# Retention of four heads among the other heads' query and gate products, in a one-core diffusion block

## The chip, the cores and the metric

The kernel runs on one NeuronCore of a Trainium2 chip. The metric is the device time of one execution in microseconds (us). The kernel before took 1373.80, 1377.99 and 1381.97 us in three runs, a median of 1377.99. In what follows PE is TensorE, DVE is VectorE, ACT is ScalarE, POOL is GpSimd, and SP is the engine that issues most DMAs.

## What is computed

One layer of a hybrid backbone over 1024 tokens of width 1024, with 256 context tokens, in float32:

```python
hx = modulate(rmsnorm(x, norm1_g), mx[0], mx[1])       # mx: six vectors of silu(c) @ w_ada
ux = hx @ w_in                                         # 3 x 512 Hyena + 4 x 512 retention columns
x0, x1, v = split(short_conv(ux[:, :1536]))            # 3 taps
y_hy = bidir_long_conv(v * x1, h, bias) * x0           # by FFT, filter h from a small MLP
q, k, vr, g = split(ux[:, 1536:], 4)                   # 8 heads x 64
q, k = rope(q), rope(k / 8)                            # pairs of neighbouring columns rotated
o = retention(q, k, vr, forward) + retention(..., backward)   # chunks of 128 tokens
y_ret = groupnorm(o) * silu(g)
x = x + mx[2] * (concat(y_hy, y_ret) @ w_out)
x = x + mx[5] * (relu(modulate(rmsnorm(x)) @ w1) ** 2 @ w2)   # the MLP, and a final rmsnorm
```

## The kernel before

Every large float32 product is done in three passes, `mm3`: each operand is split into a rounded part and a rest (`hxh`, `hxl` for the normalised input, `wh`, `wl` for weights), and high times high, high times rest and rest times high are summed in PSUM. `slab` loads a slab of 256 columns of `w_in` in two DMAs, rounds it on ACT (`A.copy`) and makes the rest on DVE; there are two buffers for `wh` and two for `wl`, so a slab's cast waits for the products of the slab before the last. `prefetch` calls it for the next slab of a list (`cols`).

A slab's product is either token-major (`token_major`: 8 token blocks x 8 x 3 = 192 matmuls of 256 columns, the weights moving) or feature-major (`feature_major`: 96 matmuls of 512 columns, the tokens moving). K, V, q and g are token-major here, the convolution inputs x1, vh and x0 are feature-major.

The code is a sequence of stages, and a scheduler lays each engine's instructions into one fixed queue: by place in the code as buffers and data allow, while what stands in `urgent()` counts as 6000 places earlier. On the chip each engine runs its own queue strictly in order, and SP issues its DMAs in order, each waiting for what its row names.

The stages, by time in the profile: 97 to 249 us K, V, filter and context; 249 to 331 the inputs of convolution half hv0; 331 to 429 the transform of hv0 with the inputs of hv1 beside it; 429 to 509 the transform of hv1 with the gate products (`pgt`) beside it; 509 to 557 the query products (`pq`); 557 to 573 a change of buffers, in which the pool of `hxh` and `hxl` is freed and one called `big` opened; 573 to 655 retention; then the second half of the output projection, and the MLP.

A transform runs through 8 residues: forward products `pXv`, a multiplication by the filter on DVE, inverse products `pGv`, copied into `Gs` by ACT. Behind the last, DVE does the inverse butterflies into `yy`. Then, for each of two blocks and two halves, `vxl` and `x0l` are loaded from memory, ACT scales `vxl`, DVE adds `yy` and multiplies by `x0l`, and SP stores the result to `mix_d`. `modulation` computes an eighth of the modulation vectors: 8 loads `adaw`, 8 DVE operations into `adac`, 4 small products `pada`.

In the retention stage `retention(hh, n, ...)` does chunk n of heads 4 hh to 4 hh + 3. It loads q rotated by `rope` (`q2l`), keys, values and states; four PE transposes (`pqd`) turn q; DVE multiplies it by decay weights (`qw`) and ACT copies it into zero-padded tiles (`sgqz`); two products give the scores (`psc`); DVE masks them (`sT`, with the masks in `tabq`); 16 narrow products (`po`) sum `vtl` with `sT` and states `stl` with `qw`. After each second chunk `out_conv` adds the convolution's share of a 128-row block of the output projection (`poh`, 24 matmuls); it reads `mx`, which `split_mix` makes from `mix_d` through `mraw`. `group_norm` follows each four chunks.

## Time and profile before

| | |
|---|---|
| median of three runs | 1377.99 us |
| the profiled execution, its own time | 1370.97 us |
| its span | 1369.2 us |
| mean granted PE clock, of full speed | 0.98 |
| busy: PE, DVE, ACT, POOL | 95%, 71%, 39%, 1% |
| chain that ended last: PE, DVE, DMA, ACT | 77%, 8%, 7%, 4% |

PE is the engine that is nearly always busy, so the span is its work and its gaps. Weight loads (PEld) overlap the matmuls. The idle time of another engine costs nothing as long as PE has a matmul that can run.

### The profile page before, as it was taken

Reading aid. Unit: us, or ns where it says so; the run is one execution under the profiler, and the core shown is the slowest. Engines: PE = TensorE matmul, PEld = TensorE weight load, DVE = VectorE, ACT = ScalarE, POOL = GpSimd, SP = SyncE. Lnnn points to the kernel's source line nnn. Section 1 sums busy time; section 2 is a strip of 40 time slices with the busy share of each in tenths; the row PEclk is TensorE's granted clock in tenths of the full one; section 3 lists DMA queues with packets and bytes.
Section 4 is the critical chain, followed back from the end, with each engine's and each line's share of the span. In section 5 each row is a group of like instructions: output and inputs, shape, how many; then the busy total and the mean of one; then the engine's idle time right before and its main releaser. Section 6 shows DMA issues by size and latency. Waiting matters only on the chain.

```text
span 1369.2 us, 20105 instructions
## 1 busy us (share of the span) xinstructions
PE 1294.8 (95%) x7386; PEld 1083.1 (79%) x7386; DVE 973.3 (71%) x1721; ACT 533.6 (39%) x912; POOL 19.4 (1%) x24
## 2 busy tenths in 40 slices
...
GB/s 374 175 151 160 233 206 212 79 228 129 169 120 215 206 162 155 270 243 182 104 96 64 251 306 326 348 302 300 238 123 232 338 321 190 193 201 185 199 79 62
DMA packets 139570, 278.19 MB, mean 203 GB/s; under 512 B 14672, under 2 KB 47056, under 8 KB 137040
## 3 DMA queue, kind: packets, MB, share of 16 engines
...
q14 instruction: 40, 0.33, 0.1%
HBM read 193.75 MB, written 83.10 MB: 202 GB/s over the span
## 4 chain that ended last, share of the span: by engine, by line
PE 77%; DVE 8%; DMA 7%; ACT 4%; issue 2%; SPq 1%; POOL 0%; DVEq 0%; ACTq 0%; POOLq 0%
PE px L184 6%; PE px L185 6%; PE px L183 6%; PE pw L183 5%; PE py L183 5%; PE py L185 5%; PE py L184 5%; PE pw L185 5%; PE pw L184 5%; DMA dft_f_k<-in_dft_f 2%; PE pga L397 1%; PE pq L185 1%; PE pq L184 1%; PE pq L183 1%; PE pGv L901 1%
## 5 line engine op out<-in xcount | busy, mean ns | idle before, releaser
L1191 DVE TENSOR_TENSOR mt<-tr,mt 128x512 fp32r<-128x512 f32 x112 | 76.6, 688 | 99.6 <-ACT mt L1190 99.4
L1190 ACT CAST mt<-tr 128x512 fp32r<-128x512 f32 x112 | 69.6, 621 | 123.5 <-PE py L185 67.1
L183 PE MATMUL px<-mt,mw 128*128 128x512 f32 (+1 forms) x320 | 112.5, 352 | 3.0 <-ACT mw L1190 2.4
L184 PE MATMUL px<-mt,mw 128*128 128x512 f32 (+1 forms) x320 | 112.5, 352 | 0.7 <-DVE mt L1191 0.7
L185 PE MATMUL px<-mt,mw 128*128 128x512 f32 (+1 forms) x320 | 111.6, 350 | 0.0
L1191 DVE TENSOR_TENSOR mw<-wr,mw 128x512 fp32r<-128x512 f32 x112 | 76.6, 686 | 4.8 <-ACT mw L1190 4.4
L183 PE MATMUL py<-mt,mw 128*128 128x512 f32 x192 | 74.7, 389 | 0.0
L184 PE MATMUL py<-mt,mw 128*128 128x512 f32 x192 | 74.7, 389 | 0.0
L185 PE MATMUL py<-mt,mw 128*128 128x512 f32 x192 | 74.7, 389 | 0.0
L1190 ACT CAST mw<-wr 128x512 fp32r<-128x512 f32 x112 | 69.0, 617 | 9.8 <-DMA wr<-in_w_mlp 5.5
L183 PEld LDWEIGHTS px<-mt,mw 128*128 128x128 f32 x320 | 61.1, 191 | 11.4 <-ACT mw L1190 2.8
L184 PEld LDWEIGHTS px<-mt,mw 128*128 128x128 f32 x320 | 61.1, 191 | 9.2 <-DVE mt L1191 1.2
L185 PEld LDWEIGHTS px<-mt,mw 128*128 128x128 f32 x320 | 60.9, 191 | 8.2 <-DVE mw L1191 0.3
L183 PE MATMUL px<-hxh,wh_x 128*128 128x512 f32 x128 | 50.7, 396 | 0.0
L184 PE MATMUL px<-hxl,wh_x 128*128 128x512 f32 x128 | 50.6, 395 | 0.0
L185 PE MATMUL px<-hxh,wl_x 128*128 128x512 f32 x128 | 50.6, 395 | 0.0
L712 DVE SCALAR_TENSOR_TENSOR adac<-adaw,cs,adac 128x512 f32<-128x512 f32 x56 | 42.9, 766 | 9.8 <-DMA adaw<-in_w_ada 9.2
L185 PE MATMUL pk<-wh_k,hxl 128*128 128x256 f32 x128 | 39.2, 307 | 3.3 <-DVE hxl L438 3.3
L184 PEld LDWEIGHTS py<-mt,mw 128*128 128x128 f32 x192 | 36.0, 188 | 7.5
L183 PEld LDWEIGHTS py<-mt,mw 128*128 128x128 f32 x192 | 36.0, 188 | 7.5
L185 PEld LDWEIGHTS py<-mt,mw 128*128 128x128 f32 x192 | 36.0, 188 | 7.4
L183 PE MATMUL pk<-wh_k,hxh 128*128 128x256 f32 x128 | 39.6, 310 | 0.4 <-ACT hxh L434 0.4
...
## 6 DMA issues: line engine op xcount, KB each, us to landing
tr<-t_d SPq DMA_DIRECT2D x112, 256.0 KB, 4.0
adaw<-in_w_ada SPq DMA_DIRECT2D x64, 256.0 KB, 4.0
WH<-in_w_mlp SPq DMA_DIRECT2D x16, 1024.0 KB, 7.4
s_d<-WH SPq DMA_DIRECT2D x16, 1024.0 KB, 5.0
wr<-s_d SPq DMA_DIRECT2D x64, 256.0 KB, 4.0
wr<-in_w_mlp SPq DMA_DIRECT2D x48, 256.0 KB, 4.2
t_d<-c SPq DMA_DIRECT2D x40, 256.0 KB, 4.1
t_d<-CH SPq DMA_DIRECT2D x40, 256.0 KB, 5.4
```

The lines of the kernel that those rows point to most:

```text
L183: PE.matmul(o, lhsT=lh, rhs=rh, start=first, stop=False, **kw)
L184: PE.matmul(o, lhsT=lh, rhs=rl, start=False, stop=False, **kw)
L185: PE.matmul(o, lhsT=ll, rhs=rh, start=False, stop=last, **kw)
L397: PE.matmul(pga[h][0:4, n, :], lhsT=cv[:, k, :], rhs=w_[:, n * 512:(n + 1) * 512], start=(k == 0), stop=(k == KC - 1 and i == 1))
L712: V.scalar_tensor_tensor(ac, wa, cs[:, k, 0:1], ac, op0=ALU.mult, op1=ALU.add)
L901: PE.matmul(o, lhsT=y[:, 0, cb], rhs=iv[:, sl[0]], start=True, stop=False)
L1190: A.copy(hi, src)
L1191: V.tensor_tensor(lo, src, hi.bitcast(F32), op=ALU.subtract)
```

## The change

**Layout.** The host permutes the columns of q and k in a head, so that rotation pairs are 32 columns apart and not neighbours. q and g become feature-major. q is then rotated by `rotate`: four DMAs of 32 x 1024 swap the halves, three DVE operations of 128 x 1024 follow, and the result goes to `q_d`. Retention loads q feature-major, twice, into rows 0 to 63 and rows 64 to 127, so the transposes and the zero-padded copies go. The scores are four products over 64 rows, in two PSUM banks.

**Order.** The convolution is cut into `conv_in` (x1, vh), `conv_gate` (x0), `conv_dft` (transforms and inverse butterflies) and `conv_out` (the loads, DVE steps and stores behind them). All five modulation pieces that stood in this region, three of them beside the gate products, stand in the convolution; `vxl` takes the buffers of another tag (`bfy`). Slabs from the seventh on are loaded from GpSimd's queue instead of SP's. After the convolution come the products of q0 and g0, then heads 0 to 3 (`heads(0, ...)`), with q1 and g1 in eight pieces of 24 matmuls, one behind each chunk. Then the pools change, and heads 4 to 7 (`heads(1, ...)`) run with one `out_conv` of 24 matmuls behind each chunk. The normed result of heads 0 to 3 goes through memory (`y_d`).

```diff
+    rc = np.concatenate([cs, cs], axis=1)
+    rs = np.concatenate([-sn, sn], axis=1)
+    c["ropeT"] = np.ascontiguousarray(np.stack([np.tile(rc.T, (2, 1)), np.tile(rs.T, (2, 1))], 1))
...
+    w = v["w_in"][0].copy()
+    for c0 in (QC, KCOL):
+        w[:, c0:c0 + 512] = w[:, c0:c0 + 512].reshape(D, NH, 32, 2).transpose(0, 1, 3, 2).reshape(D, 512)
+    a["w_in"] = w.reshape(KC, P, -1, 256).transpose(2, 1, 0, 3)
...
-            SP.dma_start(raw, src[:, ks])
+            (SP if nxt[0] < 6 else G).dma_start(raw, src[:, ks])
...
-        cols += [("x1", hv, X1C + 256 * hv), ("vh", hv, VHC + 256 * hv), ("x0", hv, X0C + 256 * hv)]
-    cols += [("g", 0, GC), ("g", 1, GC + 256), ("q", 0, QC), ("q", 1, QC + 256)]
+        cols += [("x1", hv, X1C + 256 * hv), ("vh", hv, VHC + 256 * hv)]
+    cols += [("x0", hv, X0C + 256 * hv) for hv in range(2)]
+    for hh in range(2):
+        cols += [("q", hh, QC + 256 * hh), ("g", hh, GC + 256 * hh)]
...
+    def conv_out(hv, yy):
         for b in range(2):
             blk = 2 * hv + b
             yv = yy[:, b].rearrange("p c n -> p (c n)")
             for q in range(2):
                 cc = slice(q * 512, q * 512 + 512)
-                vx = cvp.tile([P, 512], F32, tag="fx", bufs=2, name=f"vxl{blk}{q}")
+                vx = cvp.tile([P, 512], F32, tag="bfy", bufs=2, name=f"vxl{blk}{q}")
...
+    yy0 = conv_dft(0, conv_in(0))
+    for _ in range(2):
+        modulation()
+    vT1 = conv_in(1)
+    for _ in range(2):
+        modulation()
+    conv_gate(0)
+    modulation()
+    with urgent():
+        conv_out(0, yy0)
+    conv_gate(1)
+    yy1 = conv_dft(1, vT1)
+    with urgent():
+        conv_out(1, yy1)
...
-    for hh in range(2):
-        for g, ps in token_major(("g", hh), f"pgt{hh}"):
-            sg = scp.tile([P, 4, 256], F32, tag="sc", bufs=3, name=f"sg{hh}{g}")
-            with urgent():
-                A.activation(sg, ps, AF.Silu)
-                SP.dma_start(sg_d[hh][g], sg.rearrange("p n d -> p (n d)"))
-            if hh + g < 2:
-                modulation()
-        prefetch()
...
-    for hh in range(2):
-        for g, ps in token_major(("q", hh), f"pq{hh}"):
...
+    def rotate(hh, b, qf):
+
+        qs = scp.tile([P, T], F32, tag="sc", bufs=3, name=f"qs{hh}{b}")
+        for i in range(4):
+            SP.dma_start(qs[32 * i:32 * i + 32], qf[32 * (i ^ 1):32 * (i ^ 1) + 32])
+        V.tensor_tensor(qs, qs, rot[:, 1], op=ALU.mult)
+        V.tensor_tensor(qf, qf, rot[:, 0], op=ALU.mult)
+        V.tensor_tensor(qf, qf, qs, op=ALU.add)
+        SP.dma_start(q_d[hh][b * P:(b + 1) * P], qf)
+
+    def last_products():
+
+        for kind in "qg":
+            wh, wl = slabs.pop((kind, 1))
+            for b in range(2):
+                o = scp.tile([P, T], F32, tag="sc", bufs=3, name=f"{kind}f1{b}")
+                for h in range(2):
+                    ps = ps_cv(f"p{kind}1{b}{h}")
+                    cc = slice(512 * h, 512 * h + 512)
+                    for k in range(KC):
+                        mm3(ps, wh[:, k, b * P:(b + 1) * P], wl[:, k, b * P:(b + 1) * P], hxh[k][:, cc], hxl[k][:, cc],
+                            k == 0, k == KC - 1)
+                    with urgent():
+                        if kind == "q":
+                            A.copy(o[:, cc], ps)
+                            if h:
+                                rotate(1, b, o)
+                        else:
+                            A.activation(o[:, cc], ps, AF.Silu)
+                            SP.dma_start(sg_d[2 + b][:, cc], o[:, cc])
+                    yield
...
+    for b, ps in feature_major(("q", 0), "pq0"):
         with urgent():
+            qf = scp.tile([P, T], F32, tag="sc", bufs=3, name=f"qf0{b}")
+            A.copy(qf, ps)
+            rotate(0, b, qf)
+    prefetch()
+    for b, ps in feature_major(("g", 0), "pgt0"):
+        with urgent():
+            sg = scp.tile([P, T], F32, tag="sc", bufs=3, name=f"sg0{b}")
+            A.activation(sg, ps, AF.Silu)
+            SP.dma_start(sg_d[b], sg)
...
+    def retention_tables(new):
+        ctrs, sgs, tabq = [new(nm) for nm in ("ctrs", "sgs", "tabq")]
+        SP.dma_start(tabq.rearrange("p a n -> p (a n)"), tab_d.rearrange("p a h n -> p (a h n)"))
...
-        q2 = rtl.tile([P, 4, 2 * HD], F32, tag="q2", bufs=2, name=f"q2l{nm}")
-        SP.dma_start(q2.rearrange("p h d -> p (h d)"), q2_d[hh][n])
+        rtl, rtp, wqT, msk = [rt[i] for i in ("l", "p", "wqT", "msk")]
+
+        q2 = rtl.tile([P, 4, P], F32, tag="q2", bufs=2, name=f"q2l{nm}")
+        for r in range(2):
+            SP.dma_start(q2[64 * r:64 * r + 64], q_d[hh].rearrange("(h d) t -> d h t", h=4)[:, :, n * P:(n + 1) * P])
...
-        pq = ps_aux(f"pqd{nm}")
-        for h in range(4):
-            PE.transpose(pq[:, h * P:(h + 1) * P], q2[:, h], ident)
-        pqv = pq.rearrange("p (h c) -> p h c", h=4)
         qw = rtp.tile([P, 4, P], F32, tag="qw", bufs=2, name=f"qw{nm}")
-        V.tensor_tensor(qw, pqv, wqT[:, hs], op=ALU.mult)
-        qT = qz[n % 2]
-        A.copy(qT[0:64, 0:4:2], pqv[0:64, 0:4:2])
-        A.copy(qT[64:128, 1:4:2], pqv[64:128, 1:4:2])
-        pc = ps_aux(f"psc{nm}")
+        V.tensor_tensor(qw, q2, wqT[:, hs], op=ALU.mult)
+
+        pc = ps_cv(f"psc{nm}0"), ps_aux(f"psc{nm}1")
         for pr in range(2):
-            PE.matmul(pc[:, pr * 256:(pr + 1) * 256], lhsT=kt[:, pr],
-                      rhs=qT[:, 2 * pr:2 * pr + 2].rearrange("p h c -> p (h c)"), start=True, stop=True)
+            for s in range(2):
+                rows = slice(64 * s, 64 * s + 64)
+                PE.matmul(pc[s][:, pr * P:(pr + 1) * P], lhsT=kt[rows, pr], rhs=q2[rows, 2 * pr + s],
+                          start=True, stop=True)
         sT = rtp.tile([P, 4, P], F32, tag="sT", bufs=2, name=f"sT{nm}")
-        V.tensor_tensor(sT, pc.rearrange("p (h c) -> p h c", h=4), msk[:, hs], op=ALU.mult)
+        for s in range(2):
+            V.tensor_tensor(sT[:, s:4:2], pc[s][:, 0:256].rearrange("p (h c) -> p h c", h=2),
+                            msk[:, 4 * hh + s:4 * hh + 4:2], op=ALU.mult)
...
+            V.scalar_tensor_tensor(sg[:, pr], pt, gn, sg[:, pr], op0=ALU.mult, op1=ALU.mult)
+            if hh == 0:
+                SP.dma_start(y_d[pr][g], sg[:, pr])
+            else:
+                split_ret(g, blk, sg[:, pr])
...
+    def heads(hh, more):
+
+        pending = None
         for g in range(2):
-            ctr = ctrs[:, g]
-            gss = rtp.tile([P, 4, 4], F32, tag="gss", bufs=2, name=f"gss{hh}{g}")
+            ctr = rt["ctr"][:, g]
+            gss = rt["p"].tile([P, 4, 4], F32, tag="gss", bufs=2, name=f"gss{hh}{g}")
             for j in range(4):
                 retention(hh, 4 * g + j, ctr, gss)
...
                 if j == 1 and pending:
                     group_norm(*pending)
                 if j == 1:
...
+                    sg = rt["sg"][:, 2 * g:2 * g + 2]
+                    for pr in range(2):
+                        SP.dma_start(sg[:, pr], sg_d[2 * hh + pr][:, 512 * g:512 * g + 512])
+                more(g, j)
             pending = hh, g, sg, ctr, gss
-    group_norm(*pending)
+        group_norm(*pending)
...
+    open_retention()
+    retention_tables(lambda nm: rt["l" if nm == "tabq" else "p"].tile([P, 4, 512], F32, name=f"{nm}0"))
+    products = last_products()
+
+    def last_heads(g, j):
+        next(products)
+        if (g, j) == (1, 3):
+            next(products, None)
+
+    heads(0, last_heads)
+    cpool("rtp")
...
+    for k in range(4):
+        split_mix(k)
+    for d in range(KC):
+        SP.dma_start(xn[d], I["xT"][d * P:(d + 1) * P])
+
+    def projection(g, j):
+        out_conv(4 * g + j)
+        if (g, j) == (0, 1):
+            wo.append(o2)
+            for a in range(2):
+                hi, lo, raw = [t[:, 2 * a:2 * a + 2] for t in (*o2, mraw)]
+                SP.dma_start(raw, I["w_out"][2][:, 2 * a:2 * a + 2])
+                A.copy(hi, raw)
+                V.tensor_tensor(lo, raw, hi.bitcast(F32), op=ALU.subtract)
+        if (g, j) == (0, 3):
+
+            wo.append(wpool.tile([P, 4, 512], F32, tag="wh", bufs=2, name="o3r"))
+            SP.dma_start(wo[1], I["w_out"][3])
+        if (g, j) in ((0, 2), (1, 0)):
+            for i in range(2):
+                raw = mraw[:, 2 * (j // 2) + i]
+                SP.dma_start(raw, y_d[i][g])
+                split_ret(g, i, raw)
...
+    wo = []
+    heads(1, projection)
```

How this moves instructions, at three places. A row is one instruction in its engine's queue, with output and inputs; behind `waits` are the semaphores of the queues and engines it waits for.

PE, from the last gate product of its stage on. Before, the gates' last group (`pgt11`) is followed by four groups of q products (`pq00` to `pq11`) and the projection (`poh0`):

```order
L184 MATMUL pgt11_4865<-wl_g1_4117,hxh7_398 128x256
L185 MATMUL pgt11_4865<-wh_g1_4116,hxl7_406 128x256
L183 MATMUL pq00_4975<-wh_q0_4724,hxh0_391 128x256
L184 MATMUL pq00_4975<-wl_q0_4725,hxh0_391 128x256
...
L185 MATMUL pq00_4975<-wh_q0_4724,hxl7_406 128x256
L183 MATMUL pq01_5088<-wh_q0_4724,hxh0_391 128x256
...
L185 MATMUL pq11_5324<-wh_q1_4965,hxl7_406 128x256
L183 MATMUL poh0_5600<-mx00_5465,wh_o0_5201 128x512
```

Now the last product of g0 (`pgt01`) is followed by the scores and the output of chunk 0 of heads 0 to 3, and the first piece of q1 (`pq100`) stands behind these:

```order
L189 MATMUL pgt01_4746<-hxl7_406,wh_g0_4209 128x512
L190 MATMUL pgt01_4746<-hxh7_398,wl_g0_4210 128x512
L1105 MATMUL psc0_00_4835<-q2l0_0_4823,ktl0_0_4826 128x128
L1105 MATMUL psc0_01_4836<-q2l0_0_4823,ktl0_0_4826 128x128
...
L1117 MATMUL po0_0_4844<-vtl0_0_4828,sT0_0_4841 64x64 x2
L1117 MATMUL po0_0_4844<-stl0_0_4830,qw0_0_4833 64x64 x2
...
L188 MATMUL pq100_4868<-hxh0_391,wh_q1_4684 128x512
L189 MATMUL pq100_4868<-hxl0_399,wh_q1_4684 128x512
```

So the cover of four groups of products between gate and retention has moved behind the first chunk.

SP, around the last stores of the mixed channels (`mix_d`). Before, the stores of q follow, and the masks (`tabq`) and retention's first loads (`q2l0_0`) come many issues later:

```order
L982 DMA mix_d3_2963<-vxl30_4441 128x512 [waits DMAHW5_49,DVE_49]
L976 DMA vxl31_4449<-vx_d3_2959 128x512 [waits DMAHW6_49,DMAHW2_49]
L982 DMA mix_d3_2963<-vxl31_4449 128x512 [waits DMAHW1_49,DVE_49]
L1009 DMA q2_d0_4459<-q200_5072 128x2x512 [waits DVE_49]
L1009 DMA q2_d0_4459<-q202_5080 128x2x512 [waits DMAHW3_49,DVE_49]
...
L1036 DMA tabq_5463<-tab_d_1411 128x2048 [waits DMAHW2_49]
L1055 DMA mraw_5471<-mix_d0_2960 128x512 [waits DMAHW3_49]
L1055 DMA mraw_5471<-mix_d0_2960 128x512 [waits DMAHW5_49]
...
L1079 DMA q2l0_0_5499<-q2_d0_4459 128x512 [waits DMAHW0_49]
L1055 DMA mraw_5471<-mix_d3_2963 128x512 [waits DMAHW1_49,DVE_49]
```

Now masks and loads stand right behind the last two stores, which wait for DVE:

```order
L1030 DMA q_d0_4556<-qf01_4673 128x1024 [waits DMAHW7_49,DVE_49]
L992 DMA mix_d2_2962<-vxl20_4519 128x512 [waits DMAHW1_49,DVE_49]
L992 DMA mix_d2_2962<-vxl21_4527 128x512 [waits DMAHW2_49,DVE_49]
L986 DMA vxl30_4535<-vx_d3_2959 128x512 [waits DMAHW5_49,DMAHW1_49]
L986 DMA vxl31_4543<-vx_d3_2959 128x512 [waits DMAHW6_49,DMAHW2_49]
L1065 DMA sg_d1_4553<-sg01_4795 128x1024 [waits DMAHW7_49,Activation_49]
L992 DMA mix_d3_2963<-vxl30_4535 128x512 [waits DMAHW0_49,DVE_49]
L992 DMA mix_d3_2963<-vxl31_4543 128x512 [waits DVE_49]
L1077 DMA tabq0_4820<-tab_d_1411 128x2048 [waits PE_49]
L1090 DMA q2l0_0_4823<-q_d0_4556 64x4x128 [waits DMAHW3_49]
L1092 DMA ktl0_0_4826<-kT_d0_1413 128x256 [waits DMAHW5_49]
```

What moved: the masks' load has now nothing between it and the end of the convolution's output.

ACT, around the scaling of `vxl`. Before, at the end of the gate products, the first half of slab q1 is cast between a silu and the scaling for block 3:

```order
L994 ACTIVATE sg10_4831<-pgt10_4734 128x1024 [waits DMAHW2_49,PE_49,Activation_49]
L979 ACTIVATE vxl21_4433<-vxl21_4433,cols_89 128x512 [waits DMAHW3_49,DMAHW5_49,DMAHW1_49,DVE_49]
L994 ACTIVATE sg11_4962<-pgt11_4865 128x1024 [waits PE_49,Activation_49]
L206 CAST wh_q1_4965<-wr_q10_4967 128x1024 [waits DMAHW7_49]
L979 ACTIVATE vxl30_4441<-vxl30_4441,cols_89 128x512 [waits DMAHW4_49,DMAHW7_49,DMAHW1_49,DVE_49]
L206 CAST wh_q1_4965<-wr_q11_4971 128x1024 [waits DMAHW4_49]
```

Now the cast of slab g1, which waits for PE, and the silu of g0's second half stand ahead of the scaling of both halves of block 3:

```order
L1064 ACT_TABLE_LOAD [waits DMAHW5_49,DMAHW2_49,DMAHW6_49,DMAHW0_49]
L1064 ACTIVATE sg00_4743<-pgt00_4694 128x1024 [waits PE_49]
L211 CAST wh_g1_4798<-wr_g10_4800 128x1024 [waits DMASW6_49,PE_49,Activation_49]
L1064 ACTIVATE sg01_4795<-pgt01_4746 128x1024 [waits DMAHW4_49,DMAHW5_49,DMAHW3_49,DMAHW6_49,DVE_49,PE_49]
L989 ACTIVATE vxl30_4535<-vxl30_4535,cols_89 128x512 [waits DMAHW5_49,DMAHW1_49,DVE_49]
L989 ACTIVATE vxl31_4543<-vxl31_4543,cols_89 128x512 [waits DMAHW6_49,DMAHW2_49,DVE_49]
```

So those two scalings cannot begin before g0's products have ended. Farther on, ACT's queue into the projection begins before with

```order
L206 CAST wh_o0_5201<-wr_o00_5203 128x1024 [waits DMAHW0_49,PE_49,Activation_49]
L206 CAST wh_o0_5201<-wr_o01_5207 128x1024 [waits DMAHW4_49]
L206 CAST wh_o1_5626<-wr_o10_5628 128x1024 [waits DMAHW7_49,DVE_49,PE_49]
L1057 CAST mx00_5465<-mraw_5471 128x512 [waits DMAHW3_49]
L1057 CAST mx10_5467<-mraw_5471 128x512 [waits DMAHW5_49,Pool_49]
L1057 CAST mx00_5465<-mraw_5471 128x512 [waits DMAHW6_49]
L206 CAST wh_o1_5626<-wr_o11_5632 128x1024 [waits DMAHW7_49]
```

and now, with the silu of the last product of g1 (`pg111`) and both casts of slab o1 ahead of the first mixed channels (`mx00`):

```order
L211 CAST wh_o1_5448<-wr_o10_5450 128x1024 [waits DMASW2_49,PE_49]
L1050 ACT_TABLE_LOAD
L1050 ACTIVATE gf11_5349<-pg111_5421 128x512 [waits PE_49]
L211 CAST wh_o1_5448<-wr_o11_5454 128x1024 [waits DMASW3_49]
L1211 CAST mx00_5504<-mraw_5508 128x512 [waits DMAHW6_49]
L1211 CAST mx10_5506<-mraw_5508 128x512 [waits DMAHW7_49]
```

The casts of `mx` have come behind the end of the last product.

## Rows read from the trace of the kernel before

**Rows 1.** Page, part 1: busy us, share of the span, instructions of each engine.

```profile
PE 1294.8 (95%) x7386; PEld 1083.1 (79%) x7386; DVE 973.3 (71%) x1721; ACT 533.6 (39%) x912; POOL 19.4 (1%) x24
```

**Rows 2.** Stretches: length, busy us (count) by engine, clock, DMA share, GB/s.

```profile
331.00:429.00 98.00, 97.09 (x445) 80.44 (x443) 80.78 (x149) 25.09 (x36) 0.00 (x0) 1.00 0.49 157
...
557.20:572.80 15.60, 9.85 (x29) 6.76 (x30) 11.17 (x16) 4.77 (x8) 0.00 (x0) 0.78 0.73 238
572.80:655.00 82.20, 79.62 (x761) 63.22 (x759) 58.13 (x108) 24.56 (x56) 0.00 (x0) 1.00 0.69 223
```

**Rows 3.** Stretches, one tile alone: first pvh, then pq.

```profile
286.00:298.00 12.00, 12.00 (x55) 9.94 (x54) 1.34 (x2) 1.21 (x1) 1.00 0.81 259
...
512.00:552.00 40.00, 40.00 (x336) 40.00 (x335) 8.11 (x18) 1.00 0.49 169
```

**Rows 4.** PE timeline around the scores: start us, us, engine, line, operation.

```profile
634.31 1.02 PE L1098 MATMUL psc<-sgqz,ktl 128*128 128x256 f32 x4
635.17 0.60 PE L1089 MATMUL pqd<-cols,q2l 128*128 128x128 f32 x4
635.53 0.47 PE L185 MATMUL poh<-mx,wl_o 128*128 128x512 f32 x1
```

**Rows 5.** PE timeline around the narrow po products.

```profile
645.78 0.39 PE L184 MATMUL poh<-mx,wh_o 128*128 128x512 f32 x1
646.01 0.40 PE L185 MATMUL poh<-mx,wl_o 128*128 128x512 f32 x1
646.34 0.34 PE L1108 MATMUL po<-vtl,sT 128*64 128x64 f32 x4
```

**Rows 6.** Tile pqd: duration ns min/median/max, first and last start us.

```profile
L1089 PE MATMUL pqd<-cols,q2l x64: 270/273/329, 572.9 to 652.7; 128*128 128x128 f32 x64
```

**Rows 7.** DVE timeline, inverse transform of hv1: idle before in brackets.

```profile
483.09 0.69 DVE L948 TENSOR_TENSOR sd<-Gs 128x512 f32<-128x512 f32 x1 [0.50 <-ACT Gs L903]
...
496.61 0.75 DVE L980 SCALAR_TENSOR_TENSOR vxl<-yy,rinv,vxl 128x512 f32<-128x512 f32 x1
```

**Rows 8.** SP timeline: issues of the first and last mix_d store of hv1.

```profile
498.65 0.33 SPq L982 DMA_DIRECT2D mix_d<-vxl  x1
...
522.01 0.32 SPq L982 DMA_DIRECT2D mix_d<-vxl  x1
```

**Rows 9.** ACT, 429 to 560 us, by line: busy us, mean ns, idle before.

```profile
L994 ACT ACTIVATE sg<-pgt 128x1024 f32<-128x1024 f32 x4 | 4.1, 1026 | 10.4 <-PE pgt L185 10.2
L206 ACT CAST wh_o<-wr_o 128x1024 fp32r<-128x1024 f32 x3 | 3.1, 1048 | 33.5 <-PE pq L185 28.1 <-DMA wr_o<-in_w_out 5.4
L979 ACT ACTIVATE vxl<-vxl,cols 128x512 f32<-128x512 f32 x4 | 2.9, 724 | 9.8 <-DMA vxl<-vx_d 9.8
...
L994 ACT ACT_TABLE_LOAD x1 | 1.3, 1283 | 0.0
```

**Rows 10.** DMA issues: line, engine, count, KB each, median us to landing.

```profile
q2l<-q_d SPq DMA_DIRECT2D x16, 256.0 KB, 2.8
...
vxl<-vx_d SPq DMA_DIRECT2D x8, 256.0 KB, 2.9
...
mix_d<-vxl SPq DMA_DIRECT2D x8, 256.0 KB, 2.0
...
tabq<-tab_d SPq DMA_DIRECT2D x1, 1024.0 KB, 6.0
```

**Rows 11.** DVE by line: scores by mask, 572-660 us; q rotation, 509-560 us.

```profile
L1101 DVE TENSOR_TENSOR sT<-psc,tabq 128x512 f32<-128x512 f32 x16 | 11.0, 689 | 3.9 <-PE psc L1098 3.7
...
L579 DVE TENSOR_TENSOR q<-qr,rpq 128x1024 f32<-128x1024 f32 x7 | 8.5, 1215 | 0.2
```

**Rows 12.** Waits of PE, 249 to 557 us; then the DVE group of adac.

```profile
PE pGv L901 <- issue: 2.3, 2, 1.4
PE pada L715 <- DVE adac L712: 2.0, 2, 1.1
...
L712 DVE SCALAR_TENSOR_TENSOR adac<-adaw,cs,adac 128x512 f32<-128x512 f32 x56 | 42.9, 766 | 9.8 <-DMA adaw<-in_w_ada 9.2
```

207 lines of the change are left out of this document (93 added, 114 removed).

## The prediction, made before the changed kernel had run

> **What bounds the kernel now.** I read the busy totals first: TensorE (PE) is busy 1294.8 us, 95% of the span [rows 1]. So PE's program order, and every gap in it, sets the time. The second look is the table of stretches, since the whole is an average over stages [rows 2]. From 331 to 429 us, the transform of the first convolution half and the input products beside it, PE is busy 97.1 of 98.0 us and VectorE (DVE) 80.8: little to win, and a DVE near its limit. At 557.2 to 572.8 us, the change from projections to retention, it is busy 9.85 of 15.6 us at a mean granted clock of 0.78. In the retention stretch it is busy 79.6 of 82.2. Therefore the change can gain in two ways only: less PE work, or fewer gaps. It can lose by a new gap, and the third look, at the queues, is for that.
>
> **PE work taken away.** (a) The four slabs of query and gate (q, g) become feature-major: the moving operand is 512 columns wide in place of 256, with half as many matmuls. Before, 336 matmuls of pq took 40.00 us, 0.119 each; a feature-major product with 512 columns, pvh, has 55 in 12.00 us, 0.218 [rows 3]; the step from one poh to the next, also 512 columns, is 0.23 [rows 5]. I take 0.227. A slab goes from 192 x 0.119 = 22.9 to 96 x 0.227 = 21.8 us: for four slabs **-4.5 us** (-3.2 at 0.23, -8 at 0.218). (b) The four transposes of q per chunk go. The group starts at 635.17 and the next matmul at 635.53 [rows 4], so 0.36 us each; there are 64 in 16 chunks [rows 6]: **-5.8 us**. With them go two copies on ScalarE (ACT), which was not the bound. (c) The scores, psc, were two products of 256 columns over 128 rows, half of them zeros, 634.31 to 635.17, thus 0.86 us a chunk [rows 4]. They become four of 128 columns over 64 rows, into two banks. If time goes by columns alone that is again 0.86; if upper and lower row half run side by side it is 0.43, -6.9 us over 16 chunks. On the other side stands the change of shape: before the narrow po products the step between starts is 0.33 instead of 0.23 us [rows 5], 0.10 each way; one or two such excursions more per chunk are +3.2 to +6.4 us. The bounds are -6.9 and +6.4; I take **0**, the middle, since rows here decide neither.
>
> The Trainium skill (TensorEngine Tiling (Array Packing), section Key Properties) says that tiles work independently, and that a change of tiling mode drains the engine. The first would put (c) at -6.9 us and the second, by the 0.10 us of the row, back at -3.7 to -0.5; the trace agrees with a drain, and no run here shows the first.
>
> **The start of heads 0 to 3: the new wait.** This is the largest term. Let P0 be the end of the last inverse-transform product of hv1 (pGv13). Behind it PE now has 93 matmuls of g0 (21.1 us at 0.227), then the four psc0_0, then po0_0, and only then the first product of q1, so nothing can be pulled ahead of po0_0. po0_0 needs sT, and sT needs the decay masks in tabq. Before, the products of q0 and q1 stood here, 384 x 0.119 = 45.7 us of cover [rows 3], and SP issued tabq late in it. Now SP issues tabq and chunk 0's loads (q2l, ktl, vtl, stl) **behind** the two last stores of mix_d, and these wait for DVE, so the load waits for the whole output of the convolution:
> - DVE's inverse butterflies: before, from the last Gs at 483.09 to the first vxl product at 496.61, 13.5 us [rows 7]; Gs itself is some 0.8 us behind P0. Now the modulation's operations leave that stretch (-1.9 us) and three rotate operations of 1024 columns join it (3 x 1.2 us by [rows 11]): first vxl product at P0 + 16, first finished pair at P0 + 18.4.
> - One round through memory: mix_d store, reload of vxl, bias on ACT, two DVE operations, next store. Before, four stores stand 498.65 to 522.01, three rounds of 7.8 us [rows 8]. Now a round works on a pair: one more ACT operation (0.72, [rows 9]) and two more DVE operations (0.7 each), 9.9 us. Last store issued at P0 + 28.3.
> - Another chain ends nearly as late: the ACT bias stands behind the cast of slab g1 and the silu of pgt01, both of which wait for the end of g0's products: 21.1 + 1.04 + 1.03 + 2 x 0.72 [rows 9] + 2.1 on DVE + 0.4 = P0 + 27.1. It is the floor.
> - tabq, 1 MB, lands 6.0 us after its issue [rows 10], P0 + 34.6; chunk 0's q2l (2.8 us, [rows 10]) is within that. Then qw and two halves of sT, 1.4 us by the old sT's 0.69 [rows 11]: po0_0 at P0 + 36.
> PE is done with g0 and psc at 21.1 + 0.9, so it stands **14 us**; bounds 12.5 (the floor) and 18 (store and reload each 2 us slower than their medians of 2.0 and 2.9, [rows 10], since eight other transfers are on the way then). After an idle stretch the clock comes back late: in the stretch 557.2 to 572.8, behind idle time and with more of it inside, a mean of 0.78 costs 0.22 x 15.6 = 3.4 us [rows 2]. I add **3.4** (0 to 3.4).
>
> **Stage change, now after heads 0 to 3.** mraw lies where the inputs of the last product lie, so its loads wait for that product's end, and on SP they stand behind the store of the last silu (which pays a table load), the y_d stores, two xT loads and tabq; ACT's casts of mixed channels stand behind both halves of slab o1, whose second half must come through GpSimd's queue. Before, 29 matmuls, 6.7 us at 0.23, took the 15.6 us of this stretch [rows 2], 8.9 lost. Now the chain is a table load of 1.3 us and the last silu, half of 1.03 [rows 9], some 3 us of issues on SP, a load of 2.8 to 6 us like those of [rows 10], a cast and a subtraction of half a wide one each: 9 to 13 us. **+2** (-2 to +4).
>
> **Convolution and modulation.** Three pieces of modulation (each an eighth of 64 operations of 0.77 us on DVE, 6 us; [rows 12] has 56 of them) move from the g stretch to the products of the convolution inputs. In all of 249 to 557 us PE waits 2.3 us at the transforms and 2.0 on adac [rows 12]. They may go (-4) or, since DVE is at 82% in the first transform, grow: pada's six products stand earlier and the first transform products follow the transposes of v with no x0 product in between. **+3** (-4 to +8). Rope on DVE gets shorter, which gives nothing while PE is full. Slab loads from GpSimd are issued two slabs ahead and hidden.
>
> **Chunks.** In heads 0 to 3 a chunk has 24 matmuls of q1 or g1 (5.4 us) to hide its DVE and ACT steps, but they stand after po, with only two psc in front of it; in heads 4 to 7 there are 24 of poh, of which 3 to 8 stand between psc and po. **+1** (-3 to +5).
>
> **Sum.** -4.5 - 5.8 + 0 + 14 + 3.4 + 2 + 3 + 1 = **+13.1 us**. The profiled execution took 1371.0 us (span 1369.2), so 1384.1; the median of the runs shown is 1378.0, and I add the term to that: **1391 us**, main case 1383 to 1400.
>
> **The rivals.** (1) *Row halves side by side, without a drain* (not slower): decides from 0.5 us for a chunk's scores. -6.9 in place of 0, and the wait at its floor without the clock's share (12.5 in place of 17.4): -10.3 - 6.9 + 12.5 + 6 = +1.3, 1379 us. For it: the two banks and row ranges are disjoint. Against: the wait is longer than PE's gains even then, and 0.10 us at each change of shape was seen. (2) *The change does what its name says, and the wait does not come* (faster): SP's last mix_d stores are ready before g0's products end, tabq is there in time, and the moved modulation costs nothing: -10.3 alone, 1368 us. It decides from a wait under 4 us, thus tabq issued by P0 + 18; against it, DVE is only then done with the first pair. (3) *DVE is full in the transforms* (slower still): five pieces of modulation instead of two between 331 and the second transform, 3 x 6 = 18 us more DVE work beside 80.8 of 98.0; half of it uncovered, with the stage change and the wait at their upper bounds: -10.3 + 18 + 3.4 + 4 + 9 + 5 on chunks = +29, 1407 us.
>
> **How the numbers follow.** The forecast has 0.50, rival 1 0.20, rival 2 0.15 (0.13 faster, 0.02 within), rival 3 0.15. A difference of 0.5%, 7 us, is about what a measurement of this kernel can tell from none. Faster 0.13, same 0.22, slower 0.65. The range reaches from below rival 1 to rival 3: 1374 to 1408, with rival 2 and the tail of 3 left out; the main case's own is 1383 to 1400.
>
> **What would show it.** In the changed profile: PE with one gap of 12 to 18 us between the last pgt and the first po, released by DVE's sT, whose tabq is issued just after the last mix_d store; q and g slabs at 21.8 us each; no pqd; psc at 0.43 or 0.86 us a chunk; a second gap of 9 to 13 us at the first poh. It would be wrong if tabq is issued 10 us earlier than P0 + 28, if PE has other work in front of po0_0, or if the transforms lose over 8 us.

## The result, and the profile after

The changed kernel took 1397.99 us (median of four runs, 1394.62 to 1401.28), the kernel before 1379.98 us (median of four, 1373.80 to 1384.96). The ratio is 1.0147, with a 95% interval from 1.0116 to 1.0178: slower, by 18 us between the medians and 20 by the ratio. Medians and ratios are of fast executions alone, and one execution of the layout run below, at 3253.78 us, is left out of them. The forecast was 1391 us and slower. The profiled execution took 1398.15 us with a span of 1396.4 us, at a mean granted clock of 0.964 in place of 0.98.

The longest waits of PE in the two stages that the change rebuilt are the two that the prediction spoke of. Columns: engine, operation, what it waited for; total us, times, longest.

```profile
PE psc L1105 <- DMA ktl<-kT_d: 14.8, 1, 14.8
PE poh L188 <- ACT mx L1211: 14.2, 1, 14.2
```

The stretches that hold them, in the form of [rows 2] (busy us and count of PE, PEld, DVE, ACT, POOL; clock, DMA share, GB/s):

```profile
517.00:532.00 15.00, 0.31 (x2) 0.00 (x0) 5.34 (x7) 4.35 (x5) 1.06 (x2) 0.64 0.94 293
...
606.00:623.00 17.00, 1.95 (x12) 1.34 (x10) 4.06 (x6) 4.84 (x6) 0.53 (x1) 0.61 0.81 299
```

In the first, PE has only the end of its last product to do, and the DMA engines are at 94%. The second answers to 557.2 to 572.8 of [rows 2], where PE was busy 9.85 of 15.6 us; now it is busy 1.95 of 17. The transposes (pqd, [rows 6]) are gone, and the four slabs of q and g take 87.2 us at their usual step (384 matmuls at 0.227 us, for 768 at 0.120 before), 5.0 less.

**The wait at the start of heads 0 to 3.** PE around it (start us, us, operation, idle time before and what ended it):

```profile
495.83 0.58 PE L188 MATMUL pgt<-hxh,wh_g 128*128 128x512 f32 x1
...
516.92 0.39 PE L190 MATMUL pgt<-hxh,wl_g 128*128 128x512 f32 x1
532.12 1.22 PE L1105 MATMUL psc<-q2l,ktl 64*128 64x128 f32 x8 [14.81 <-DMA ktl<-kT_d]
533.87 0.48 PE L1117 MATMUL po<-vtl,sT 128*64 128x64 f32 x4 [0.53 <-issue]
```

What SP issues behind the transforms, and then DVE's part:

```profile
513.85 0.92 SPq L992 DMA_DIRECT2D mix_d<-vxl  x2
514.82 0.95 SPq L988 DMA_DIRECT2D x0l<-x_d  x2
515.87 0.93 SPq L986 DMA_DIRECT2D vxl<-vx_d  x2
...
522.53 1.00 SPq L992 DMA_DIRECT2D mix_d<-vxl  x2
523.59 0.50 SPq L1077 DMA_DIRECT2D tabq<-tab_d  x1
524.13 1.43 SPq L1090 DMA_DIRECT2D q2l<-q_d  x2
525.60 0.60 SPq L1092 DMA_DIRECT2D ktl<-kT_d  x1
```

```profile
511.81 1.41 DVE L990 SCALAR_TENSOR_TENSOR vxl<-yy,rinv,vxl 128x512 f32<-128x512 f32 x2
...
520.49 1.42 DVE L990 SCALAR_TENSOR_TENSOR vxl<-yy,rinv,vxl 128x512 f32<-128x512 f32 x2 [1.02 <-ACT vxl L989]
...
531.73 0.69 DVE L1099 TENSOR_TENSOR qw<-q2l,tabq 128x512 f32<-128x512 f32 x1 [4.92 <-DMA q2l<-q_d]
533.35 0.76 DVE L1109 TENSOR_TENSOR sT<-psc,tabq 128x256 f32<-128x256 f32 x2 [0.92 <-PE psc L1105]
```

P0, where the last inverse product gives way to the next gate product, is at 495.83. The first vxl product starts at P0 + 16.0, the second pair of stores is issued at P0 + 26.7, the masks right behind, and the first po starts at P0 + 38.0. The wait is put down to ktl, which landed at 531.99, after the masks (530.78); but ktl was issued only at 525.60, last but a few of a row that begins with the stores. Store, reload, bias, product, store, masks and chunk loads stand one behind the other.

**The stage change behind heads 0 to 3.** SP first, then ACT and PE:

```profile
609.37 0.33 SPq L1051 DMA_DIRECT2D sg_d<-gf  x1
609.79 0.87 SPq L1144 DMA_DIRECT2D y_d<-sgs  x2
610.72 1.64 SPq L1236 DMA_DIRECT2D XN<-in_xT  x2
612.39 1.44 SPq L1077 DMA_DIRECT2D tabq<-tab_d  x1
613.94 2.25 SPq L1209 DMA_DIRECT2D mraw<-mix_d  x4
```

```profile
622.06 2.56 ACT L1211 CAST mx<-mraw 128x512 fp32r<-128x512 f32 x4 [5.53 <-DMA mraw<-mix_d]
```

```profile
622.73 0.80 PE L188 MATMUL poh<-mx,wh_o 128*128 128x512 f32 x1 [14.21 <-ACT mx L1211]
```

The last gate product began at 606.19. SP stands at the store of the last silu until 609.37, and the raw mixed channels (mraw) leave last, at 613.94, behind 2 MB of residual rows and masks. They land 8.1 to 8.3 us later.

### The profile page after: what moved, and what is told of

Same layout as the page of the kernel before. It is cut to its first block, busy times and chain, and to the rows that moved or that the text cites. A ratio compares the mean times of both kernels' runs of the same rounds, so it can differ in the third digit from the quotient of the medians.

```text
span 1396.4 us, 19368 instructions
## 1 busy us (share of the span) xinstructions
PE 1294.1 (93%) x7002; PEld 1063.0 (76%) x7002; DVE 968.9 (69%) x1719; ACT 532.0 (38%) x892; POOL 30.1 (2%) x44
## 4 chain that ended last, share of the span: by engine, by line
PE 77%; DMA 8%; DVE 7%; ACT 4%; issue 2%; SPq 1%; POOL 0%; ACTq 0%; DVEq 0%; POOLq 0%
PE px L190 6%; PE px L189 6%; PE px L188 6%; PE py L188 5%; PE py L189 5%; PE py L190 5%; PE pw L188 5%; PE pw L190 5%; PE pw L189 5%; PE poh L188 1%; PE pga L404 1%; PE po L1117 1%; PE poh L189 1%; PE poh L190 1%; PE pq L188 1%
## 5 line engine op out<-in xcount | busy, mean ns | idle before, releaser
L188 PEld LDWEIGHTS px<-mt,mw 128*128 128x128 f32 x320 | 60.9, 190 | 11.7 <-ACT mw L1285 3.1
```

Of the source, the lines that this page charges most:

```text
L188: PE.matmul(o, lhsT=lh, rhs=rh, start=first, stop=False, **kw)
```

## The experiments

Each ratio is to the kernel before, run beside it on the same chip; the changed kernel's is 1.0147. Twelve kernels were run. Of the single edits to the changed kernel, only the early masks have an interval clear of the changed kernel's 1.0116 to 1.0178. Query products as cover, stores together, urgent raw loads and the moved modulation overlap it, so their times alone prove no gain. The traces help where they share a fixed point: up to the last inverse product (P0) the changed kernel's PE queue is the same in six of the runs, and these six edits move no matmul ahead of it. P0 is at 495.8 us in the changed kernel's profiled execution and at 484.6 to 490.3 in the six; from P0 to the end the changed kernel takes 900.6 us.

### Query products ahead of chunk 0 as cover

```diff
+    next(products)
+    next(products)
     def last_heads(g, j):
-        next(products)
-        if (g, j) == (1, 3):
-            next(products, None)
+        next(products, None)
```

> The changed kernel, with the first two pieces of q1 (48 matmuls, 10.9 us) put ahead of chunk 0 of heads 0 to 3 instead of behind chunks 0 and 1; chunks 6 and 7 then have no piece behind them. If the idle 14.8 us in front of the first scores is only missing cover, it falls to some 4 us, the slow clock behind it (3.3 us) mostly goes, and the last two chunks lose up to 3 us each: 1398 - 14 + 5 = about 1389 us. If PE waits there for something that comes later when more work is in front (the loads queue behind other loads, or DVE is the bound), the gap stays over 10 us and the time is 1396 to 1400.

Measured: 1391.39 us, 1.0119 (1.0088 to 1.0149). The wait hardly shrank:

```profile
PE psc L1105 <- DMA stl<-st_d: 13.3, 1, 13.3
PE pz L1139 <- DVE ctrs L1135: 11.3, 1, 11.3
```

```profile
518.13 0.45 SPq L1077 DMA_DIRECT2D tabq<-tab_d  x1
518.62 0.64 SPq L1090 DMA_DIRECT2D q2l<-q_d  x1
519.37 2.48 SPq L1026 DMA_DIRECT2D qs<-qf  x4
...
527.40 0.46 SPq L1097 DMA_DIRECT2D stl<-st_d  x1
```

The products did run earlier, 10.9 us of them. But their results have DMAs of their own: the swaps of q (qs) now stand between chunk 0's loads on SP, and the last of stl, issued 3.9 us behind tabq in the changed kernel (527.51), leaves 9.3 us behind it. The products are missing at the end, where the last chunks' normalisation (pz) waits 11.3 us. Cover that is moved brings its transfers along. From P0 to the end this kernel takes 904.7 us, 4 more than the changed one: what its profiled execution gained stands ahead of P0, where the edit moved no matmul.

### Masks and chunk 0's loads early

Four heads' masks and chunk 0's loads get their own buffers, in place of the modulation's, and are issued before the last stores:

```diff
     conv_gate(1)
+    cpool("adp")
+    tabp = opool("tabp")
+    tab0 = tabp.tile([P, 2, 4, P], F32, name="tab0")
+    SP.dma_start(tab0, tab_d[:, :, 0:4])
     yy1 = conv_dft(1, vT1)
...
+        rtl = tabp if (hh, n) == (0, 0) else rtl
+        early = tc.high_priority(offset=12000) if (hh, n) == (0, 0) else ExitStack()
```

> The changed kernel, with the masks of heads 0 to 3 and chunk 0's loads in buffers of their own (in place of the modulation's, closed earlier), so that SP issues them ahead of the last mix_d stores; the rest of its order is kept. If the SP queue alone holds chunk 0 back, the idle time in front of the first scores and output falls from 15.7 to under 3 us, and the time to about 1381. If DVE's order (the scaling of block 3 and the rest of slab g1 ahead of the mask step) ends nearly as late, 8 to 10 us of idle time stay, in front of po0_0 instead of psc0_0, and the time is 1391 to 1394.

Measured: 1387.69 us, 1.0081 (1.0056 to 1.0105). The scores are now early, and another link of the chain holds po:

```profile
517.26 1.22 DVE L212 TENSOR_TENSOR wl_g<-wr_g,wh_g 128x1024 fp32r<-128x1024 f32 x1 [2.45 <-ACT wh_g L211]
518.41 0.75 DVE L1126 TENSOR_TENSOR sT<-psc,tab 128x256 f32<-128x256 f32 x2
```

```profile
518.97 0.48 PE L1135 MATMUL po<-vtl,sT 128*64 128x64 f32 x4 [9.56 <-DVE sT L1126]
```

The masking of scores (sT) stands on DVE behind a slab's rest (wl_g), whose cast waits for its weights. Of 15.7 us of wait some 6 were the masks' place; the order on DVE is the rest. From P0 to the end the kernel takes 894.3 us, 6.3 less than the changed one.

### The last block's stores together

```diff
-                vx = cvp.tile([P, 512], F32, tag="bfy", bufs=2, name=f"vxl{blk}{q}")
+                own = blk == 3
+                vx = cvp.tile([P, 512], F32, tag=f"pr{q + 1}" if own else "bfy", bufs=1 if own else 2, name=f"vxl{blk}{q}")
-                x0 = cvp.tile([P, 512], F32, tag="fx", bufs=2, name=f"x0l{blk}{q}")
+                x0 = cvp.tile([P, 512], F32, tag="yraw" if own else "fx", bufs=2, name=f"x0l{blk}{q}")
```

> The changed kernel, in which the last block's loads of convolved and plain mixed channels have buffers of their own, so that the second pair of loads doesn't wait for the first pair's products; all four stores of mixed channels then stand together, about 20 to 22 us behind the last transform's product and not at 26.7, and the mask loads and chunk 0's loads behind them. Theory (the wait of 14.8 us at the start of heads 0 to 3 is the chain of loads, products, stores and masks, one after the other on SP): the wait falls by 5 to 6 us to 8 to 10 us and the time with it, to about 1391 to 1393 us, 1.010 of the kernel before. Rival (ACT's silu and copies, which end about as late as the masks land, or the landing of chunk 0's loads hold the first scores): the wait falls by less than 2 us and the time stays at 1396 to 1399 us.

Measured: 1390.17 us, 1.0105 (1.0076 to 1.0135). The time came out as the theory had it, but not by its mechanism. All four stores stand together from 509.95, and tabq is issued 23 us behind the last inverse product instead of 27.8; but the wait at psc fell only to 12.7 us. Now tabq, the chunk's loads, a half slab of weights and the last silu's store are on the queues at once, and chunk 0's q2l lands after 8.7 to 9.1 us where it took 6.8 to 7.2 in the changed kernel. Of 4.6 us that SP gained, the transfers gave back more than half. From P0 to the end the two kernels take the same, 900.5 and 900.6 us. The whole difference between the two profiled executions stands ahead of P0, where the edit moved no matmul; that the stores alone gain time is not shown.

### Raw mixed channels urgent

```diff
-    for k in range(4):
-        split_mix(k)
+    with urgent():
+        for k in range(4):
+            split_mix(k)
```

> The changed kernel, with the loads and splits of the mixed channels for the projection (split_mix) marked urgent, so that SP issues the first four ahead of the loads of x and of the second table. If the 14.2 us of idle time in front of the first poh is the queue of transfers ahead of mraw (2 MB of x and masks at 320 GB/s are 6 us), it falls to 6 to 8 us and the time to about 1391. If it is the cast of slab o1's second half on ACT (it ended at 616.5, 6 us before the first mx cast), it falls to 8 to 9 us only; if neither, 1396 to 1400.

Measured: 1388.48 us, 1.0109 (1.0066 to 1.0152). mraw left at 606.36, 5.9 us behind the last gate product in place of 7.3, ahead of tabq but still behind the silu's store, two y_d stores and two residual rows; poh waited 11.7 us in place of 14.2. So 2.5 us of the 14.2 were the place behind the masks. From P0 to the end the kernel takes 895.9 us, 4.7 less than the changed one.

### The layout alone, and the raw tile's place

The changed layout (feature-major q and g, no transposes, paired scores) in the order of the kernel before:

```diff
+    for hv in range(2):
+        vT = conv_in(hv)
+        conv_gate(hv)
+        modulation()
+        conv_out(hv, conv_dft(hv, vT))
...
+    cols += [("g", 0, GC), ("g", 1, GC + 256), ("q", 0, QC), ("q", 1, QC + 256)]
```

> Only the first half of the change: the order of the kernel before (x1, vh, x0 of each half, modulation where it was, g then q, then buffers change and all eight heads with the projection between), with the new layout: q and g feature-major, rotate, no transposes, scores on half rows. If the forecast's work terms hold (-4.5 for the slabs, -5.8 for the transposes, 0 for the scores), it is 10 us faster than before, a ratio of 0.992 to 0.993; with the scores at 0.65 us a chunk, as heads 4 to 7 of the changed kernel show, 13 us, 0.990. If the gain is lost again to the swaps of q through memory or to drains, the ratio is 0.997 to 1.003.

Measured: 1378.67 us, 1.0033 (1.0008 to 1.0058). The time is no shorter. Of PE's work some 8 us are gone and not 14, counted as the steps from start to start without idle time: the slabs and the transposes take 10.5 us less, but the scores cost what they cost before (14.5 us for 14.2). In about half of the chunks the products of the two row halves stand apart here, and each half then takes 0.64 us, as long as both do side by side. The rest is lost to waits: poh waits 11.4 us for mx, and some 12 us are lost in 655 to 677 us, at the end of the retention. There the raw tile lay over the last hidden channels. The next run puts it where the kernel before has it:

```diff
+    tabq_ = place(10, "tabq", F32)
+    mx = [[place(2 * h + i, f"mx{h}{i}") for i in range(2)] for h in range(2)]
+    retention_tables(lambda nm: tabq_ if nm == "tabq" else place(spare[nm], nm, F32))
+    mraw = place(13, "mraw", F32)
```

> The changed kernel's layout of slabs, transposed products and paired scores in the order of the kernel before, as in the run of the layout alone (1380.8 us, 1.0033 of the kernel before), with one difference: the raw mixed channels and the mixed slabs lie where the kernel before has them, and not over the last tile of hidden channels. In that run TensorE's work had shrunk by about 14 us and poh waited 11.4 us for the mixed slabs, whose raw loads wait for the gate products' last read. Theory (the place of the raw tile decides the start of the output products, there and in the changed kernel): the raw load is issued during the products, the wait of 11.4 us for mx falls under 3 us, and the time is 1369 to 1375 us, 0.994 to 0.999 of the kernel before. Rival (the output products wait for the loads that share the queues, whatever the place): the wait stays over 8 us and the time is 1378 to 1384 us, about 1.003.

Measured: 1382.56 us, 1.0059 (1.0037 to 1.0081), and the same wait. The rival holds; the theory of the place, which I had formed on the changed kernel's trace, falls. SP's row, and PE:

```profile
552.87 0.34 SPq L210 DMA_DIRECT2D wr_o<-in_w_out  x1
553.25 0.43 SPq L1046 DMA_DIRECT2D tabq<-tab_d  x1
553.73 0.43 SPq L1143 DMA_DIRECT2D mraw<-mix_d  x1
```

```profile
PE poh L188 <- ACT mx L1145: 11.5, 2, 10.4
```

mraw needs nothing of PE here, and leaves 3 us behind the last product all the same: it stands on SP behind a half slab of weights (wr_o) whose buffer comes free only with that product.

### The modulation as before

```diff
     yy0 = conv_dft(0, conv_in(0))
-    for _ in range(2):
-        modulation()
+    modulation()
     vT1 = conv_in(1)
-    for _ in range(2):
-        modulation()
-    conv_gate(0)
     modulation()
+    conv_gate(0)
```

The other three pieces stand behind the two blocks of q0 and the first block of g0, thus beside the products of heads 0 to 3.

> The changed kernel with the modulation where the kernel before has it: two pieces before the sixth and after the last block of the convolution's gate, three between the query and gate products of heads 4 to 7, in place of all five beside the convolution. Theory (the convolution and the transforms lose 17.5 us to waits and the slower clock after the change, 7.7 before, because of the modulation's products and loads among them): these stretches get back 5 to 8 us, the wait at the start of heads 0 to 3 stays at 14 to 16 us, and the time is 1389 to 1393 us, about 1.009 of the kernel before. Rival (the losses come from the output weights' loads and casts, not from the modulation): the same losses of 17 us or so and 1396 to 1400 us, about 1.0147, or more, if the three pieces' weight loads hold up the loads of heads 0 to 3.

Measured: 1394.67 us, 1.0152 (1.0115 to 1.0189): no gain. In 240 us to the last inverse product, steps beyond the usual ones and idle time sum to 10.5 us in place of 17.6, which looks like the theory's 5 to 8 us. But the run with urgent raw loads, which leaves the modulation alone, lost only 9.9 us there, so the difference need not come from this edit (the part on the convolution below says more). The start of heads 0 to 3 got longer, since the pieces' small products wait on DVE and the scores wait longer:

```profile
PE psc L1105 <- DMA ktl<-kT_d: 16.3, 1, 16.3
PE pada L718 <- DVE adac L715: 4.8, 2, 2.9
```

### Query products ahead of the gate products

The layout run with the raw tile's place, and

```diff
-    cols += [("g", 0, GC), ("g", 1, GC + 256), ("q", 0, QC), ("q", 1, QC + 256)]
+    cols += [("q", 0, QC), ("q", 1, QC + 256), ("g", 0, GC), ("g", 1, GC + 256)]
```

with the two loops of products in the same order.

> The kernel of the run on the raw tile's place (changed layout, order and places of before), in which the query products of each half of the heads come ahead of the gate products, so that rotation, stores and swaps of the queries run beside the gate products and not ahead of the scores. Theory (with the layout alone the gain of 14 us of TensorE's work is lost where the retention waits for the queries): the waits at the start of each retention fall by some 5 us and the time is 1360 to 1370 us, 0.988 to 0.996 of the kernel before. Rival (the gate's casts, stores and the mixed slabs are then late at the other end, and the output products wait by as much): 1372 to 1382 us, 0.997 to 1.004.

Measured: 1372.05 us, 0.9968 (0.9952 to 0.9985): at the lower end of the rival's range, and outside the theory's. It is ahead of both kernels, by 0.3% of the one before: rotation, swaps and stores of q run beside the gate products. poh still waits 9.4 us for mx. That wait was the next to try, in this kernel with the raw loads urgent, and the masks more so, to keep these ahead:

```diff
-    retention_tables(lambda nm: tabq_ if nm == "tabq" else place(spare[nm], nm, F32))
+    with tc.high_priority(offset=7000):
+        retention_tables(lambda nm: tabq_ if nm == "tabq" else place(spare[nm], nm, F32))
...
-    for k in range(4):
-        split_mix(k)
+    with urgent():
+        for k in range(4):
+            split_mix(k)
```

> The kernel with the query products ahead of the gate products (1372.1 us, 0.9968 of the kernel before), in which the loads of raw mixed channels and their splits are urgent: SP issues seven of eight... of them behind the masks and ahead of the last half slab of output weights, and not behind that slab's issue, which waits for a cast. Theory (what holds the output products at the stage change, 9.4 us there, 14.2 in the changed kernel, is where the loads stand in SP's row, not the layout or the place of the tiles): the first raw load leaves 8 us or more earlier, the wait of poh falls under 3 us, and the time is 1362 to 1367 us, 0.989 to 0.993 of the kernel before. Rival (the loads that are on the queues together, masks, raw channels and weights, land no sooner for being issued sooner): the wait stays at 7 us or more and the time at 1369 to 1375 us.

Measured: 1374.37 us, 0.9989 (0.9971 to 1.0006). poh waits 7.8 us; the rival holds, but not for its reason. mraw left at 559.43, 2.5 us behind the last product, since SP stood at the store of the last silu until 559.01, as in the changed kernel. Behind whichever waiting row it stands, being urgent helps little.

So the loads were given to POOL's queue, which is empty there, with no other edit to the kernel with q first:

```diff
-            SP.dma_start(raw, mix_d[k][:, cc])
+            G.dma_start(raw, mix_d[k][:, cc])
```

> The kernel with the query products ahead of the gate products (order and places of the kernel before, layout of the changed one; 1372.1 us, 0.9968 of the kernel before), in which POOL's queue, empty there, issues the loads of raw mixed channels, so that they leave once the stores they read have landed and not behind SP's store of the last silu. There poh waited 9.4 us. Theory (SP's row holds the raw loads): the first four leave 5 us or more before the last gate product ends and have landed by its end; poh then waits for the casts alone, 1 to 3 us, with 2 to 3 us more behind it for the second four; the time is 1364 to 1368 us, 0.991 to 0.995. Rival (the loads, wherever issued, collide with the masks and the weights, and the half slab of weights or the masks come late instead): poh waits 7 us or more or another wait takes its place, and the time is 1370 to 1375 us.

Measured: 1372.42 us, 0.9982 (0.9959 to 1.0004). POOL's issues and PE's longest waits:

```profile
540.69 2.22 POOL L1143 DMA_DIRECT2D mraw<-mix_d  x4 [443.40 <-PE pgt L190]
555.19 2.34 POOL L1143 DMA_DIRECT2D mraw<-mix_d  x4 [12.29 <-DVE mx L1146]
```

```profile
PE poh L188 <- ACT mx L1145: 4.6, 2, 2.7
```

This shows the cause of the wait: with the first four loads 11 us ahead of the last product's end, the 9.4 us become 2.7, and 1.9 for the second four. The time did not follow. poh starts 5.5 us earlier than in the kernel with q first, the last poh ends 3.5 us earlier, and the first product of the normalisation behind the output projection (ptr) starts 0.6 us earlier (689.1 against 689.7). In between, the last chunks of the retention stand on their own loads and DVE steps, and PE has no other work. That is so with q first as well (first row), and with the loads on POOL (second row) it only begins sooner:

```profile
630.00:660.00 30.00, 25.26 (x249) 0.78 0.46 134
630.00:660.00 30.00, 25.66 (x228) 0.73 0.46 128
```

(PE busy us and count, clock, DMA share, GB/s.) In the 30 us before, PE is busy 30.00 and 28.76 us. The gain became a wait and a slower clock at the other end of the stage.

### The edits together

Masks early, stores together, raw loads urgent, and the raw tile off the hidden channels, in the changed kernel:

> The changed kernel with three earlier edits together: four heads' masks and chunk 0's loads early in buffers of their own (alone 1.0081 of the kernel before), the last block's stores of mixed channels together (alone 1.0105), the loads of raw mixed channels urgent (alone 1.0109), and the raw tile not over the last tile of hidden channels. Theory (the three losses are separate: the wait at the start of heads 0 to 3, the round ahead of it, the stage change): the gains add, 9 + 6 + 5 us off the changed kernel's 1398, so 1376 to 1382 us, 1.000 to 1.004 of the kernel before, with under 8 us of wait at the first scores and under 10 at poh. Rival (they share one bound, the loads' bytes between the last transform and the first scores or DVE's row there): no more than the best alone, 1386 to 1390 us.

Measured: 1372.42 us, 0.9979 (0.9960 to 0.9999). By the ratios the edits give 9.1, 5.8 and 5.2 us alone and 23.2 together; from P0 to the end, by the traces, 6.3, 0.1 and 4.7 alone and 18.1 together (882.5 us for 900.6). By the ratios the 3 us beyond the sum are within the noise; by the traces the edits give more together than alone. The raw tile's place was not tried alone here; mraw leaves 5.8 us behind the last gate product, where it left at 5.9 with urgent loads alone, so the place changed nothing there. What is left of the two waits:

```profile
PE poh L188 <- ACT mx L1230: 11.8, 1, 11.8
PE po L1136 <- DVE sT L1127: 1.9, 2, 1.5
PE psc L1121 <- DMA q2l<-q_d: 1.8, 2, 1.5
```

The first wait is all but gone. With the stores together, the slab's rest that stood ahead of sT on DVE in the run with early masks comes behind it. The order of the changed kernel is thus no worse than the one before, once the first chunk's inputs don't queue behind the convolution's output. Last, the same with the raw loads on POOL and the residual rows later:

```diff
-            SP.dma_start(raw, mix_d[k][:, cc])
+            G.dma_start(raw, mix_d[k][:, cc])
...
     def projection(g, j):
+        if (g, j) == (0, 0):
+            for d in range(KC):
+                SP.dma_start(xn[d], I["xT"][d * P:(d + 1) * P])
         out_conv(4 * g + j)
```

> The changed kernel with the earlier edits together (masks and chunk 0's loads early, the last block's stores together, raw loads urgent, 1372.4 us, 0.998 of the kernel before), in which POOL's queue issues the loads of raw mixed channels, behind the last half slab of output weights, and the residual rows are loaded after the first output product has been written. In the run without this poh waited 11.8 us: SP held the raw loads until 590.2, 6.0 us behind the last gate product, since it stands at the store of a silu and at two stores of the retention's result. Theory (the issue on SP is what is late): the raw loads leave 2 to 4 us sooner, with no residual rows beside them, poh waits 7 to 9 us, and the time is 1367 to 1370 us, 0.994 to 0.997. Rival (the landing is what is late, whichever queue issues): poh waits 11 us or more and the time stays at 1371 to 1374 us.

Measured: 1384.27 us, 1.0059 (1.0031 to 1.0088): slower by 11 us, on which neither theory had counted.

```profile
PE poh L188 <- ACT mx L1230: 8.9, 1, 8.9
PE psc L1121 <- DMA ktl<-kT_d: 6.2, 2, 5.5
```

poh waits less, as the theory had it. POOL issues mraw in order behind a slab's load (588.55, then 589.39), 3.5 us behind the last gate product in place of 5.8 on SP. But these four loads land 6.7 to 9.4 us after their issue, beside masks and chunk loads, which themselves take up to 14.4 us; and the next scores, which now stand ahead of most of the first output block's products, wait 5.5 us for ktl. Whether the later residual rows or POOL's queue did this, one run with both can't tell.

## Why the prediction was right

**The forecast of slower, and its main term, held.** The wait came at the start of heads 0 to 3, for the reason given and of nearly the size: 14.8 us ahead of psc and 0.9 behind it, for 14. Its links, from P0: the first vxl product at 16.0 (16 predicted), the last store at 27.3 (28.3), the masks landed at 35.0 (34.6), po at 38.0 (36). The last store came 1.0 us sooner than the sum of a round said, and the masks took 7.2 us instead of 6.0, with chunk 0's loads beside them. One link is not as predicted: the sum had psc done right behind g0's products, chunk 0's loads landed within the masks' time, and the wait between psc and po. In the trace ktl landed 1.2 us after the masks, PE waited ahead of psc, and the scores came behind the wait. The early masks take some 6 us of the wait away and the edits together nearly all of it, and both shorten the time clear of the noise, so the chain is shown and not only argued; the stores together take 2.1 us of the wait and show no time of their own. The clock behind the wait cost some 2.6 us against 3.4: PE was at half speed from 532.1 to 538.2 and idle for 0.9 of that, and psc took 1.22 us where it takes 0.72 at full speed.

**PE's work.** Slabs -5.0 for -4.5, transposes -5.8 as predicted. The scores, taken at 0, are 0.65 us a chunk in most of heads 4 to 7, where they were 0.86 [rows 4]. In heads 0 to 3 they are some 0.8, since they stand in groups of 12, 8 and 4 matmuls and not of 8 a chunk, so that the two row halves are often apart: in sum about -1. The shape change costs 0.10 us behind them, as the prediction had bounded it.

**The step that failed: the stage change.** It was taken at +2 with an upper bound of 4, from a chain of 9 to 13 us; from the end of the last gate product to the first poh it is 16.1. By idle time and lengthened steps it lost about 17 us where the kernel before lost about 10: +7. The links were named, but a load was priced at 2.8 to 6 us from the medians of [rows 10], and it took 8.1 to 8.3 with 2 MB of residual rows and masks issued ahead of it; SP's issues in front of it took 4.6 us from 609.37 to 613.94, not 3; and the last silu was done 2.8 us behind its product, not 1.8, since ACT had a cast of slab o1 ahead of it. The urgent loads take 2.5 us of the wait away, and in the order of the kernel before an issue well ahead (the raw loads on POOL, q first) takes most of it. In the changed order POOL's queue took 2.9 of 11.8 us and cost more elsewhere, so there the rest is not shown to be removable. The prediction's reason for the late issue (the raw tile's place) is not the one that decides: without it, in the layout run with the place of before, the wait is the same, and with the edits together it is that of the urgent loads alone (11.8 and 11.7 us).

**Convolution and modulation, +3 (-4 to +8).** In the profiled execution the losses up to the last inverse product grew from 6.4 to 17.6 us, outside the bounds; by the prediction's own sign (over 8 us) that would make it wrong here. But the run with urgent raw loads has word for word the same PE queue up to the output products, and lost 9.9 us there: +3.5. The difference is the clock. Length, PE busy us and count, clock, DMA share, GB/s; the changed kernel first, then that run:

```profile
280.00:290.00 10.00, 10.00 (x34) 0.72 0.64 180
...
436.00:440.00 4.00, 3.70 (x13) 0.50 0.57 206
```

```profile
280.00:290.00 10.00, 10.00 (x46) 1.00 0.67 187
...
436.00:440.00 4.00, 4.00 (x19) 1.00 0.38 137
```

Both have nearly the same waits at pada just before, 1.7 and 2.6 us in the changed kernel and 1.5 and 2.5 in that run. Of the six runs that share the PE queue up to P0, the stores together have both stretches at half speed as well (275.6 to 282.4 and 432.6 to 439.4), three runs have one of 3.4 us, and two have none. So some 7 us of the 27 between the two profiles come and go from one execution to the next, whatever was edited. How much of the 18 us between the medians that is, stays open: the profiled execution of the changed kernel took the median of its runs, while the one of the kernel before took 7 us less than the median of three. The term lies between +3.5 and +11.2.

**Chunks, +1 (-3 to +5).** Counted in steps beyond the usual ones and idle time, heads 0 to 3 lose some 7 us more than the products that stood there before (some 0.55 us in front of po in four of the chunks, 2.3 at one sT, and the clock behind it), while heads 4 to 7 and the second half of the output projection lose some 10 less: about -3, the lower bound.

Together the terms as measured give -11.8 + 15.7 + 2.6 + 7 + 11.2 - 3 = +21.7, where ptr starts 25.3 us later in the trace (715.94 against 690.66); some 3.6 us I could not place. With +3.5 for the convolution the sum is +14, beside 18 between the medians. That the forecast's +13 comes near is in part luck: the wait and the stage change were 6.7 us dearer than predicted, and PE's work and the chunks 5.5 us cheaper.

**The rivals.** That the wait would not come (1368) is refuted. Row halves side by side (1379) was half right as to the hardware and wrong in its sum. DVE full in the transforms (1407) did not happen: DVE went from 80.8 to 86.9 us of the 98.0 of [rows 2], and PE lost only 1.0 us there (96.1 busy for 97.1).
